# One hybrid decoder block on one core: when the rotary angles, tables and k's rotation are issued

## The chip, the cores and the metric

The kernel runs on one core of one Trainium2 chip. A core has a matrix engine (TensorE, here PE, with its weight loads as PEld), a vector engine (VectorE, DVE), a scalar engine (ScalarE, ACT), GpSimd (POOL) and a sync engine (SyncE, SP), which in this kernel issues nearly all DMA transfers. Each engine works through its own instruction list strictly in the order in which the program wrote it, and waits where an operand is not there yet. The metric is the device time of one execution in microseconds (us); lower is better.

## The reference

One decoder block in float32: RMSNorm with adaptive shift and scale, one large input projection, a sliding-window attention branch with rotary positions and learned sinks, a gated spatial branch with a LayerNorm, a gated merge, and an output projection with a second norm. Cut to what the change touches:

```python
def _rope(t, positions):
    inv_freq = ROPE_THETA ** (-jnp.arange(half) / half)
    ang = positions[..., None] * inv_freq
    cos, sin = jnp.cos(ang)[:, :, None, :], jnp.sin(ang)[:, :, None, :]
    t1, t2 = t[..., :half], t[..., half:]
    return jnp.concatenate([t1 * cos - t2 * sin, t2 * cos + t1 * sin], -1)
...
    h = _rms(x, g_pre) * (1.0 + scale) + shift
    q, k, v, z_a, u_b, v_b, z_b, g_logits = jnp.split(h @ w_in, SPLIT_IDX, -1)
    q, k = _rope(q, positions), _rope(k, positions)
...
    vn = _layernorm(v, ln_g, ln_b)      # v: gelu of v_b, in the gated spatial branch
```

The sequence is 2048 long and the model is 1024 wide; q has 8 heads and k and v have 2, of 64 columns each. All arrays are float32.

## The kernel before

**Products.** Every big matrix product is a Strassen-like scheme: for a pair of output column tiles seven half-size products stand in place of eight (`p` = 0 to 6). Each operand is split in a rounded high part and a low part, and one product is 12 matmuls of 128x512 (4 slices of the contraction, three of high-high, high-low and low-high each; `mm3`, L170). So a product needs a weight tile `W` (high by ACT, L223; low by DVE, L158, through `w_of` and `low_now`) and a moving tile `T` (high by ACT, L392 or L782; low by DVE, L803 and others). The sequence is done in two halves of 1024 (`s` = 0 and 1).

**The order of the work.** The program is written out product by product. `step` counts a slot up after each product; the text calls it the product's number, from 0. `later(n, f)` puts `f` in front of the product that is n slots on, `later(n, f, True)` behind its matmuls, and "mid" in their middle. Nothing is reordered afterwards: where `f` is called, its instructions enter the engines' lists.

**Products 0 to 27** are the first four pairs of the first half, done product by product over all four pairs at once: products 0 to 3 use moving tile `T[0]`, 4 to 7 `T[1]`, 8 to 11 `T[2]`, 12 to 15 `T[3]` (the fourth), 16 to 19 `T[4]`, 20 to 23 `T[5]`, 24 to 27 `T[6]`. In this stretch DVE also builds the moving tiles (L704, L762, L158) and sums the weight tiles. From product 28 on each pair takes seven products in a row: 28 to 34, 35 to 41, 42 to 48 and so on, in the four PSUM banks X, W, Y and Z.

**Rotary tables.** `rope_steps` (L583) is a generator of 21 short steps that reduce position times frequency to an angle; `rope_do(1)` runs one. Nine of them (DVE at L593, L623, L632, L590, L637; one of them is two ACT instructions, L625 and L626) run behind products 9 to 17. `rope_out` (L639) turns both angle tiles into sine and cosine on ACT and stores them to DRAM (`cs_s`, L646); the sine function needs a table that ACT loads first (ACT_TABLE_LOAD). `load_rope` (L861) loads them back as four tiles, sine and cosine for each half of the 1024 columns; each is four small DMAs on SP (L868, 32x512, called row loads below).

**k's rotation.** Pair 2 yields k (and v). Its results are stored raw (`kr_s`); `rope_finish` (L947) loads them again (L954, and L958 with rows swapped), multiplies by sine on POOL (`psub`, L161) and by cosine on DVE (L962), adds (L164), rounds (ACT, L966), takes the low part (L158) and stores (L990).

**LayerNorm of v_b.** `ln_step` (L920) loads a 128x512 block (SP, L923), PE transposes it behind a later product (L929, 4 matmuls of 128x128), then statistics and the norm follow on DVE (L933, L934, L941) with a power on POOL (L154, L155). For i = 0, 1, 2, 3 the load is called ahead of product 27, 29, 32, 34, and the transposes stand behind product 31, 33, 36, 38.

**Evacuation.** At p = 4 of a pair DVE adds bank Y to a kept tile (L436, shown as L164) and so frees bank Y, into which product p = 6 writes.

Of the kernel before, what the change touches and what calls it, by code (L numbers as in the profile page):

```python
# [50 lines left out]
NFIRST = 4  # L51
# [4 lines left out]
def hybrid_block(ctx: ExitStack, tc: tile.TileContext, xt, x, wada, wgate, wI, wP, wO,  # L56
# [30 lines left out]
    def flat(tag, dt=F32):  # L87
        return t2(tag, [P, 512], dt)
# [10 lines left out]
    def dram(name, shape):  # L99
        return tc.dram_tile(shape, F32, name=name)  # L100
# [16 lines left out]
    kr_s = [dram(f"kr{i}", [P, TG]) for i in range(2)]  # L117
# [39 lines left out]
    def sub(o, a, b):  # L157
        dve.tensor_tensor(out=o, in0=a, in1=b, op=ALU.subtract)  # L158

    def psub(o, a, b, op=ALU.subtract):  # L160
        pool.tensor_tensor(out=o, in0=a, in1=b, op=op)  # L161

    def add(o, a, b):
        dve.tensor_tensor(out=o, in0=a, in1=b, op=ALU.add)  # L164
# [64 lines left out]
    def later(n, f, post=False):  # L229
        hooks.setdefault((slot[0] + n, post), []).append(f)  # L230
# [419 lines left out]
    def rope_do(n):  # L650
        for _ in range(n):
            next(rope_it, None)
# [208 lines left out]
    def load_rope(s, ns):  # L861

        def one(h, i, key):
            g = 2 * s + h
            t = flat("m")
            for r in range(4):
                at = 64 * (r // 2) + r % 2
                sp.dma_start(t[at : at + 64 : 2, :] if at < 64 else t[at:P:2, :], cs_s[i][32 * g : 32 * (g + 1), :])  # L868
            if key == "s":
                later(3, lambda: act.activation(out=t, in_=t, func=AF.Copy, scale=col[:, C_SGN : C_SGN + 1]))  # L870
            ropet[key, h] = t
        for h in range(2):
            for i, key in enumerate("cs"):
                later(ns[2 * h + i], lambda h=h, i=i, key=key: one(h, i, key))
# [32 lines left out]
    def ft(key):  # L907
        return int(key[0]) - 1
# [38 lines left out]
    def rope_finish(h, R, put_out, wait, raw=None):  # L947
        st = {}

        def turn():  # L950
            nonlocal R
            if raw is not None:
                R = flat("x")
                sp.dma_start(R, raw)  # L954
            st["hi"] = flat("x", F32R)
            st["rot"] = st["hi"].bitcast(F32)
            for r in range(2):
                sp.dma_start(st["rot"][r:P:2, :], (R if raw is None else raw)[1 - r : P : 2, :])  # L958

        def mix():  # L960
            psub(st["rot"], st["rot"], ropet["s", h], ALU.mult)
            dve.tensor_tensor(out=R, in0=R, in1=ropet["c", h], op=ALU.mult)  # L962

        def both():
            add(R, R, st["rot"])
            act.copy(st["hi"], R)  # L966

        def low():
            sub(R, R, st["rot"])
        later(1 + wait, turn)  # L970
        later(5 + wait, mix)
        later(6 + wait, both, True)
        later(8 + wait, low)
        later(9 + wait, lambda: put_out(st["rot"], R))
# [8 lines left out]
    def ev_kv(s):  # L983
        def ev(key, src, psum):
            h = half(key)
            if ft(key) == 0:
                def put_out(hi, lo):
                    ks = slice(P + s * NT + h * 512, P + s * NT + (h + 1) * 512)
                    for i, t in enumerate((hi, lo)):
                        sp.dma_start(k_s[:, i, ks], t)  # L990
                R = rope_in(src, psum, "e")
                if s == 0:
                    store(1, kr_s[h], R)
                rope_finish(h, R, put_out, (15, 9)[h] if s == 0 else h, kr_s[h] if s == 0 else None)
            else:
                t = src
                if psum:
                    t = flat("e")
                    act.copy(t, src)

                def turn():
                    b = bank()
                    for c in range(4):
                        pe.transpose(b[:, c * P : (c + 1) * P], t[:, c * P : (c + 1) * P], ident)

                    def out_():
                        o = flat("qS"[s])
                        act.copy(o, b)
                        at = 1 + s * 8 + h * 4
                        store(1, v_s[:, at : at + 4, :], o.rearrange("p (a b) -> p a b", a=4))  # L1010
                    later(1, out_)
                later((3, 10)[h] if s == 0 else 2, turn, True)
        return ev
# [309 lines left out]
    def run_all():  # L1323
        nonlocal T

        for s in range(NS):
# [6 lines left out]
            if s == 0:  # L1333
                later(26, setup_sgu)
                later(28, zero_heads)
            load_rope(s, ((29, 28, 31, 30), (10, 11, 12, 13))[s])
            for i in range(8):
                later((27 + 5 * i // 2, 17 + 3 * i)[s], lambda i=i: ln_step(s, i))
            for c in range(4):
# [25 lines left out]
            if s == 0:  # L1365
# [50 lines left out]
                later(2 * NFIRST, fetch_all, True)  # L1416
                later(NFIRST, lambda: sp.dma_start(mcpt, mcp))
                later(NFIRST, lambda: sp.dma_start(snk8, sinks.broadcast_to([P, 8])))
                for i in range(9):
                    later(9 + i, lambda: rope_do(1), True)  # L1420
                later(26, rope_out, "mid")
                later(12, lambda: dve.tensor_scalar(out=snk8, in0=snk8, scalar1=1.0 / SM, scalar2=None, op0=ALU.mult))
                for p in range(3, 7):
                    for i, (n, post) in enumerate(((-4, True), (-3, False), (-3, True), (-2, False), (-2, True), (-1, False))):
# [218 lines left out]
```

## Time and profile before

| | us |
|---|---|
| three executions: median (lowest to highest) | 1201.62 (1200.4 to 1201.99) |
| the profiled execution | 1203.53 |
| its span, first to last instruction | 1201.8 |
| PE busy in the span | 1184.4 |
| mean granted clock of PE, share of full speed | 0.997 |

PE is busy nearly all the time, so the reading is of its short gaps: a timeline of PE shows where a product starts later than the one before it allows, and the timelines of DVE, ACT and SP show what it waited for. In a timeline a row merges neighbouring instructions of the same form: start, time from its start to its end, engine, line, operation, operands, count, and in brackets the idle time before it with the instruction that ended it. Matmuls of a row overlap the next row's first ones by some 0.15 us, so products are counted from start to start.

### The profile page before, as it was taken

What the parts mean: (1) busy time and instruction counts of PE and PEld (TensorE: products, weight loads), DVE (VectorE), ACT (ScalarE), POOL (GpSimd) and SP (SyncE); (2) the same over time, 40 slices, a digit from 0 to 9 for tenths busy, and PEclk for the clock granted to TensorE, in tenths of its full rate; (3) what the DMA queues carried; (4) which work ended last, traced back from release to release, by engine and by line L of the source; (5) the groups of instructions that cost most, each with busy time, mean ns of one, the idle gap of its engine ahead of it and who ended that gap; (6) DMA issues with size and microseconds to landing.
All of it is one profiled execution on the core that took longest, in us unless ns stands there. A gap on an engine that the chain in (4) does not pass through costs nothing.

```text
span 1201.8 us, 17373 instructions
## 1 busy us (share of the span) xinstructions
PE 1184.4 (99%) x5440; PEld 945.6 (79%) x5440; DVE 869.2 (72%) x1320; ACT 644.0 (54%) x1379; POOL 342.4 (28%) x290
## 2 busy tenths in 40 slices
PE   8999999999999999999999999999999999999997
PEld 4677878888777777888888887777778878888886
DVE  6897688678876676355866886554877977767775
ACT  5476455568765685443444766555845412444443
POOL 0001455333365201112201113130042301255453
PEclk9999999999999999999999999999999999999999
DMA  9546898959899997868779998998968987846352
GB/s 354 232 150 205 268 358 316 279 162 296 258 329 347 310 318 271 279 221 263 254 233 278 269 292 244 317 306 254 330 199 287 383 262 261 290 149 191 129 179 88
DMA packets 228548, 312.78 MB, mean 260 GB/s; under 512 B 20964, under 2 KB 103012, under 8 KB 228456
## 3 DMA queue, kind: packets, MB, share of 16 engines
q1 hardware_dynamic: 227984, 310.99, 79.5%
q8 instruction: 43, 0.70, 0.2%
q14 instruction: 49, 0.40, 0.1%
q0 software_dynamic: 176, 0.53, 0.1%
q10 hardware_dynamic: 296, 0.16, 0.1%
HBM read 201.82 MB, written 105.06 MB: 255 GB/s over the span
## 4 chain that ended last, share of the span: by engine, by line
PE 83%; DVE 6%; DMA 5%; ACT 2%; issue 2%; SPq 1%; POOL 0%; ACTq 0%; DVEq 0%; POOLq 0%
PE bankY L175 27%; PE bankX L175 19%; PE bankW L175 11%; PE bankZ L175 11%; PE b L175 3%; PE s L175 2%; PE b L1168 2%; PE s L1118 1%; PE s L1119 1%; DMA raw<-in_wP 1%; PE b L1057 1%; DVE W L158 1%; PE b L1153 1%; DMA raw<-sS 1%; DVE e L164 1%
## 5 line engine op out<-in xcount | busy, mean ns | idle before, releaser
L175 PE MATMUL bankY<-T,W 128*128 128x512 f32 x1566 | 383.2, 393 | 2.6 <-DVE e L164 2.3
L175 PEld LDWEIGHTS bankY<-T,W 128*128 128x128 f32 x1566 | 291.7, 188 | 64.3 <-issue 3.7
L158 DVE TENSOR_TENSOR W<-raw,W 128x512 fp32r<-128x512 f32 x327 | 268.5, 827 | 73.4 <-ACT W L223 70.5
L223 ACT CAST W<-raw 128x512 fp32r<-128x512 f32 x327 | 201.8, 618 | 131.0 <-PE b L175 41.9
L175 PE MATMUL bankX<-T,W 128*128 128x512 f32 x1098 | 266.9, 391 | 0.1
L175 PEld LDWEIGHTS bankX<-T,W 128*128 128x128 f32 x1098 | 204.2, 188 | 41.9 <-DVE T L803 0.5
L175 PE MATMUL bankW<-T,W 128*128 128x512 f32 x672 | 165.7, 393 | 2.9 <-DVE T L158 2.0
L175 PE MATMUL bankZ<-T,W 128*128 128x512 f32 x672 | 163.8, 391 | 0.0
L175 PEld LDWEIGHTS bankW<-T,W 128*128 128x128 f32 x672 | 124.4, 188 | 32.7 <-DVE T L158 3.5
L175 PEld LDWEIGHTS bankZ<-T,W 128*128 128x128 f32 x672 | 124.9, 188 | 27.2 <-ACT T L392 1.6
L161 POOL TENSOR_TENSOR S<-x,x 128x512 f32<-128x512 f32 x28 | 37.1, 1329 | 239.1 <-DMA x<-yb 107.8
L161 POOL TENSOR_TENSOR raw<-raw,raw 128x512 f32<-128x512 f32 x46 | 73.9, 1606 | 93.1 <-DVE W L158 44.3
L161 POOL TENSOR_TENSOR S<-raw,raw 128x512 f32<-128x512 f32 x23 | 34.9, 1518 | 168.8 <-DMA raw<-in_wI 74.5
L158 DVE TENSOR_TENSOR T<-x,T 128x512 fp32r<-128x512 f32 (+1 forms) x105 | 73.6, 748 | 3.6 <-ACT T L392 3.6
L164 DVE TENSOR_TENSOR e<-bankY,e 128x512 f32<-128x512 f32 x43 | 29.7, 690 | 59.2 <-PE bankY L175 59.0
L175 PE MATMUL b<-T,W 128*128 128x512 f32 x282 | 69.7, 390 | 0.5 <-DVE W L158 0.5
L175 PEld LDWEIGHTS b<-T,W 128*128 128x128 f32 x282 | 52.8, 188 | 11.8 <-DVE W L158 0.9
L175 PE MATMUL s<-T,W 128*128 128x512 f32 x246 | 60.1, 389 | 0.2 <-DVE e L164 0.2
L392 ACT CAST T<-x 128x512 fp32r<-128x512 f32 x100 | 56.0, 619 | 3.8 <-PE s L175 2.1
L175 PEld LDWEIGHTS s<-T,W 128*128 128x128 f32 x246 | 46.1, 188 | 10.2 <-issue 0.6
L161 POOL TENSOR_TENSOR raw<-S,raw 128x512 f32<-128x512 f32 x23 | 32.7, 1424 | 70.1 <-DVE W L158 58.5
L1147 ACT ACTIVATE P<-P,rc 128x128 f32<-128x128 f32 x128 | 44.5, 396 | 11.6 <-DVE rc L1143 11.6
(292 smaller groups left out, 1459.0 us busy)
## 6 DMA issues: line engine op xcount, KB each, us to landing
raw<-in_wI SPq DMA_DIRECT2D x127, 256.0 KB, 4.6
raw<-sS SPq DMA_DIRECT2D x92, 256.0 KB, 5.0
g<-e SPq DMA_DIRECT2D x64, 256.0 KB, 4.1
sS<-raw SPq DMA_DIRECT2D x43, 256.0 KB, 4.4
T<-in_wada SPq DMA_DIRECT2D x16, 512.0 KB, 8.2
q<-q SPq DMA_DIRECT2D x64, 128.0 KB, 5.4
q<-k_s SPq DMA_DIRECT2D x64, 128.0 KB, 4.9
raw<-m SPq DMA_DIRECT2D x32, 256.0 KB, 4.1
```

The source lines that it names most:

```text
L158: dve.tensor_tensor(out=o, in0=a, in1=b, op=ALU.subtract)
L161: pool.tensor_tensor(out=o, in0=a, in1=b, op=op)
L164: dve.tensor_tensor(out=o, in0=a, in1=b, op=ALU.add)
L175: pe.matmul(o, w[:, i, sl], t[:, j, kt, :], start=start and kt == kts[0] and n == 0, stop=stop and kt == last and n == 2, skip_group_check ...
L223: act.copy(w[:, 0, :], src)
L392: act.copy(T[p][:, 0, kt, :], rs[kt])
L1057: pe.matmul(b[:, ch * P : (ch + 1) * P], st["v", h][:, ch, :], wT[:, c, :], start=True, stop=True)
L1118: pe.matmul(o, q[:, g, :], k[:, 0, :], start=True, stop=False)
L1119: pe.matmul(o, q[:, g, :], k[:, 1, :], start=False, stop=True)
L1147: act.activation(out=st["P", kv][:, g, 0:P], in_=st["P", kv][:, g, 0:P], func=AF.Copy, scale=st["rc", kv][:, g : g + 1])
L1153: pe.transpose(t[:, g * P : (g + 1) * P], st["P", kv][:, g, 0:P], ident)
L1168: pe.matmul(o[own, :], v[:, k, own], st["pv", kv][k], start=k == 1, stop=k == 0)
```

## The change

- The nine angle steps run behind products 13 to 21 in place of 9 to 17.
- `low_now` is called once more, ahead of product 9: the low part of the weight tile of product 11 is then issued at once, ahead of two of the vector instructions that prepare the fourth moving tile.
- `rope_out` runs in the middle of product 24 in place of 26.
- The four table loads of the first half are called ahead of products 27, 26, 29, 28 in place of 29, 28, 31, 30.
- `rope_finish` for k in the first half starts two products sooner (wait 13 and 7 in place of 15 and 9).

```diff
-                rope_finish(h, R, put_out, (15, 9)[h] if s == 0 else h, kr_s[h] if s == 0 else None)
+                rope_finish(h, R, put_out, (13, 7)[h] if s == 0 else h, kr_s[h] if s == 0 else None)
...
-            load_rope(s, ((29, 28, 31, 30), (10, 11, 12, 13))[s])
+            load_rope(s, ((27, 26, 29, 28), (10, 11, 12, 13))[s])
...
+                later(2 * NFIRST + 1, low_now)
                 for i in range(9):
-                    later(9 + i, lambda: rope_do(1), True)
-                later(26, rope_out, "mid")
+                    later(13 + i, lambda: rope_do(1), True)
+                later(24, rope_out, "mid")
```

The number of instructions is the same on every engine but ACT, which loads a function table 35 times in place of 34 (the added one stands ahead of the first exponential of the attention, L1138). PE's list is the same. Names below carry tile numbers that shift with the order of allocation.

DVE's list before, from the second of the four instructions (L704) that scale the source of the fourth moving tile; `W_794` is the weight tile of product 11, `W_839` that of product 12:

```order
L704 SCALAR_TENSOR_TENSOR x_357<-x_357,AS,e_489 128x512
L593 SCALAR_TENSOR_TENSOR T_321<-T_321 128x512
L704 SCALAR_TENSOR_TENSOR x_358<-x_358,AS,e_489 128x512
L803 SCALAR_TENSOR_TENSOR T_823<-x_356,AS,T_823 128x512
L158 TENSOR_TENSOR W_794<-x_406,W_794 128x512
L158 TENSOR_TENSOR W_839<-S_830,W_839 128x512
```

DVE's list of the change from the same place, where the weight tile of product 12 is `W_838`:

```order
L158 TENSOR_TENSOR W_794<-x_406,W_794 128x512
L704 SCALAR_TENSOR_TENSOR x_357<-x_357,AS,e_489 128x512
L704 SCALAR_TENSOR_TENSOR x_358<-x_358,AS,e_489 128x512
L803 SCALAR_TENSOR_TENSOR T_824<-x_356,AS,T_824 128x512
L158 TENSOR_TENSOR W_838<-S_830,W_838 128x512
```

The low part of product 11's weights went up by four places, and the angle step L593 went out to a later place.

ACT's list before, from the weight cast of product 27; `m_1002` and `m_1001` are the two angle tiles, L916 is the gelu that empties bank W:

```order
L223 CAST W_1177<-raw_1062 128x512
L916 ACTIVATE e_1192<-bankW 128x512
L223 CAST W_1195<-raw_1085 128x512
L916 ACTIVATE e_1210<-bankZ 128x512
L223 CAST W_1216<-S_1213 128x512
L643 ACT_TABLE_LOAD
L643 ACTIVATE m_1002<-m_1002 128x512
L645 ACTIVATE m_1001<-m_1001,col 128x512
```

ACT's list of the change from the same cast:

```order
L223 CAST W_1177<-raw_1057 128x512
L643 ACT_TABLE_LOAD
L643 ACTIVATE m_1100<-m_1100 128x512
L645 ACTIVATE m_1099<-m_1099,col 128x512
L916 ACT_TABLE_LOAD
L916 ACTIVATE e_1196<-bankW 128x512
L223 CAST W_1199<-raw_1081 128x512
L916 ACTIVATE e_1214<-bankZ 128x512
```

The two sines stand four instructions further up, with a table load on either side of them.

SP's list before, from the first of the four sets of row loads (L868); `q_1308` is the LayerNorm block i = 1, and L954 and L958 load k's first half:

```order
L868 DMA m_1274<-cs_315 32x512 x4
L254 DMA sS_1_95<-raw_1085 128x512
L911 DMA g_0_254<-e_1261 128x512
L868 DMA m_1303<-cs_314 32x512 x4
L923 DMA q_1308<-vb_302 128x4x128
L246 DMA raw_1335<-in_wI 128x512
L868 DMA m_1337<-cs_315 32x512 x4
L1192 DMA S_1342<-in_x 128x512
L1192 DMA S_1344<-in_x 128x512
L954 DMA x_1346<-kr_312 128x512
L958 DMA x_1348<-kr_312 64x512 x2
```

SP's list of the change from the third set of row loads on (the first two stand further up); `q_1323` is the same LayerNorm block:

```order
L868 DMA m_1284<-cs_315 32x512 x4
L954 DMA x_1289<-kr_312 128x512
L958 DMA x_1291<-kr_312 64x512 x2
L254 DMA sS_1_95<-raw_1081 128x512
L911 DMA g_0_254<-e_1271 128x512
L868 DMA m_1318<-cs_314 32x512 x4
L923 DMA q_1323<-vb_302 128x4x128
L246 DMA raw_1351<-in_wI 128x512
```

All four sets of row loads and the three loads of k's first half now stand ahead of the LayerNorm block i = 1, where two sets stood before.

## Rows read from the trace of the kernel before

**Rows 1.** The page: busy time of each engine with its share of the span.

```profile
PE 1184.4 (99%) x5440; PEld 945.6 (79%) x5440; DVE 869.2 (72%) x1320; ACT 644.0 (54%) x1379; POOL 342.4 (28%) x290
```

**Rows 2.** Timeline of PE: first row of products 11, 12, 16, 17, 24 and 25.

```profile
68.04 0.61 PE L175 MATMUL b<-T,W 128*128 128x512 f32 x2
...
71.52 2.88 PE L175 MATMUL bankX<-T,W 128*128 128x512 f32 x12
...
82.40 2.43 PE L175 MATMUL bankW<-T,W 128*128 128x512 f32 x10
...
85.86 2.92 PE L175 MATMUL bankZ<-T,W 128*128 128x512 f32 x12
...
105.29 1.87 PE L175 MATMUL bankW<-T,W 128*128 128x512 f32 x7
...
109.78 2.89 PE L175 MATMUL bankZ<-T,W 128*128 128x512 f32 x12
```

**Rows 3.** Timeline of PE: the transposes of LayerNorm block i = 1, and products 34, 40, 41 and 42.

```profile
136.61 0.60 PE L929 MATMUL b<-cst,q 128*128 128x128 f32 x4
136.97 2.98 PE L175 MATMUL bankY<-T,W 128*128 128x512 f32 x12
...
154.35 2.88 PE L175 MATMUL bankZ<-T,W 128*128 128x512 f32 x12
159.56 4.44 PE L175 MATMUL bankY<-T,W 128*128 128x512 f32 x12 [2.34 <-DVE e L164]
...
164.33 3.01 PE L175 MATMUL bankX<-T,W 128*128 128x512 f32 x12
```

**Rows 4.** Busy time of each engine in two stretches of 2 us, with the count of instructions, PE's granted clock (PEclk, 1.00 is 2.4 GHz and 0.50 is 1.2 GHz), the busy share of the DMA engines and GB/s.

```profile
157.00:159.00 2.00, 0.23 (x2) 0.00 (x0) 1.97 (x5) 0.00 (x0) 0.07 (x1) 1.00 1.08 392
161.00:163.00 2.00, 2.00 (x7) 1.51 (x6) 2.00 (x4) 0.19 (x1) 1.37 (x2) 0.50 1.06 341
```

**Rows 5.** The same view for the two stretches in which DVE builds the moving tiles; the busy times are of PE, PEld, DVE, ACT and POOL in this order.

```profile
65.00:90.00 25.00, 24.08 (x106) 19.20 (x105) 24.61 (x42) 19.08 (x31) 0.00 (x0) 1.00 0.50 168
90.00:109.00 19.00, 18.08 (x77) 13.82 (x75) 18.57 (x27) 10.48 (x18) 3.48 (x2) 1.00 0.63 208
```

**Rows 6.** Timeline of DVE: the low parts of the weights of products 11 and 12, an angle step with idle time ahead of it, and the last low part of the seventh moving tile.

```profile
68.37 0.69 DVE L158 TENSOR_TENSOR W<-x,W 128x512 fp32r<-128x512 f32 x1
69.05 0.69 DVE L158 TENSOR_TENSOR W<-S,W 128x512 fp32r<-128x512 f32 x1
...
77.07 0.69 DVE L593 SCALAR_TENSOR_TENSOR T<-T 128x512 f32<-128x512 f32 x1 [0.39 <-ACT T L626]
...
108.47 0.68 DVE L158 TENSOR_TENSOR T<-x,T 128x512 fp32r<-128x512 f32 x1
```

**Rows 7.** Timeline of ACT: the cast of the weights of product 12, that of product 27, the sines' table load, the first sine, and a copy out of bank Z behind the first exponentials, where the change adds a table load.

```profile
68.39 0.62 ACT L223 CAST W<-S 128x512 fp32r<-128x512 f32 x1 [1.10 <-DMA S<-in_wI]
...
110.33 0.60 ACT L223 CAST W<-raw 128x512 fp32r<-128x512 f32 x1
...
113.83 1.28 ACT L643 ACT_TABLE_LOAD   x1
115.13 0.63 ACT L643 ACTIVATE m<-m 128x512 f32<-128x512 f32 x1
...
233.25 0.57 ACT L445 COPY bankZ<-bankY 128x512 f32<-128x512 f32 x1 [0.85 <-PE bankY L175]
```

**Rows 8.** Timeline of SP's issues: the two table stores, LayerNorm block i = 0, the first set of row loads, block i = 1, the third set, the loads of k's first half, the fourth set.

```profile
115.79 0.93 SPq L646 DMA_DIRECT2D cs<-m  x2
...
117.72 0.76 SPq L923 DMA_DIRECT2D q<-vb  x1
...
122.46 2.42 SPq L868 DMA_DIRECT2D m<-cs  x4
...
128.45 0.59 SPq L923 DMA_DIRECT2D q<-vb  x1
...
129.75 2.36 SPq L868 DMA_DIRECT2D m<-cs  x4
...
133.24 0.43 SPq L954 DMA_DIRECT2D x<-kr  x1
133.72 1.12 SPq L958 DMA_DIRECT2D x<-kr  x2
...
135.99 2.63 SPq L868 DMA_DIRECT2D m<-cs  x4
```

**Rows 9.** Time from issue to landing in us, lowest, median and highest: of the six LayerNorm loads between 110 and 165 us, then of block i = 1 alone; and, with the median in the last column, of the v_b stores and the table stores between 110 and 120 us and of the row loads between 118 and 165 us.

```profile
DMA to landing us min/median/max: 2.9/4.5/5.3
...
DMA to landing us min/median/max: 3.9/3.9/3.9
...
vb<-e SPq DMA_DIRECT2D x2, 256.0 KB, 4.3
cs<-m SPq DMA_DIRECT2D x2, 256.0 KB, 3.8
...
m<-cs SPq DMA_DIRECT2D x16, 64.0 KB, 2.4
```

**Rows 10.** Timeline of DVE: the statistics of LayerNorm block i = 1, and the add that empties bank Y ahead of product 41.

```profile
139.73 0.69 DVE L933 BATCH_NORM_STATS2 bst<-b 128x6 f32<-128x512 f32 x1
...
158.76 0.66 DVE L164 TENSOR_TENSOR e<-bankY,e 128x512 f32<-128x512 f32 x1
```

## The prediction

> **What bounds the kernel now.** I read the page first: PE is busy for 1184.4 of 1201.8 us [rows 1], so a change pays only where it closes or opens one of PE's gaps. Next I read PE's timeline from start to start. A product that nothing delays takes 2.72 us to the next one's start, and a group of four 128x128 transposes 0.36 (136.61 to 136.97) [rows 3]. By that measure product 11 loses 71.52 - 68.04 - 2.72 = 0.76 us, product 16 loses 0.74 and product 24 loses 1.77 [rows 2]. Product 41 should start at 154.35 + 2.72 = 157.07 and starts at 159.56, 2.49 late, with DVE's add as the releaser. From there to product 42, with one group of transposes between, 4.77 us pass where 3.08 would do, 1.69 too many [rows 3]. The windows say why: in the wait PE has 0.23 of 2 us busy, and two us after its end the granted clock is 0.50, the 1.2 GHz level [rows 4]. So this one wait costs 4.18 us in all. Last I read what stood behind each of them: the lists of DVE, ACT and SP.
>
> **Angle steps and the extra low part.** They move work on DVE, which in this stretch is the bound: 24.61 of 25 us busy from 65 to 90, 18.57 of 19 from 90 to 109 [rows 5]. Product 11's weights get their low part at 68.37 [rows 6], and product 11 waits for it. The order shows it four places earlier, so the 0.76 at product 11 goes, and with the angle steps out of the way so does the 0.74 at 16. But the moving steps and the low part stay on the same engine, and all nine angle steps still come ahead of the last low part of the seventh tile (108.47), which holds product 24. From the scaling of the fourth tile to there DVE has the same 67 instructions in both lists. The end of that row of work, not the waits within it, sets product 25. So the 1.50 us reappear as a longer wait at product 24, about 1.77 + 1.50 = 3.3.
>
> What is left is how DVE's idle time changes. It was 0.39 + 0.43 = 0.82 over the two stretches [rows 5], and 0.39 of that is one angle step that waits for ACT's pair [rows 6]. With the step L593 (0.69) no longer ahead, DVE reaches the low part of product 12 at about 69.05 - 0.69 = 68.36, while its cast runs from 68.39 to 69.01 [rows 7]: some 0.56 new. ACT's angle pair comes to stand ahead of the fifth-group tile's cast, an estimated 0.55 by the pair's two instructions, the nearest row being that 0.39. Net +1.11 - 0.39 = +0.7 if the other 0.43 stays, +0.3 if a later DVE finds those operands ready. I take +0.3, since DVE is the later one at each of them; bounds -0.8 (all old idle gone, none new) and +0.7. Product 25 then starts 0.3 later.
>
> **Sines and row loads.** ACT's list shows the sines directly behind product 27's cast, which ended at 110.93 [rows 7]. With the 0.3, the table load of 1.28 and a sine of 0.63 the first sine is done near 113.2 (before: 115.76). Its store is issued at once, as it was (115.79) [rows 8], and lands 3.8 later [rows 9], near 117.1. There SP begins the first set of row loads, which began at 122.46 before [rows 8].
>
> The price stands on SP. LayerNorm block i = 1, issued at 128.45 before, has all four sets and k's three loads ahead of it now: one more set of 2.36, another of 2.63, and 0.43 + 1.12 for k's loads [rows 8], 6.5 us with their gaps of about 0.1 each some 6.8. To count it from the new start: SP issues two sets, and between them a v_b store and a weight load of some 0.4 each, and comes to block i = 0 at 117.1 + 4.8 + 0.8 = 122.7. That block waits for the v_b store, issued near 119.8 and 4.3 in landing [rows 9]: it goes out at 124.1, done at 124.9. From its end to block i = 1 passed 128.45 - 118.48 = 9.97 before [rows 8], two sets among them; now the same stretch holds two sets again, and k's loads, 1.6 with their gaps: 124.9 + 10.0 + 1.6 = 136.5. I take 136.4; bounds 133 (by 128.45 + 6.8 less what the earlier start gives back, without the wait for the store) and 137.
>
> The block landed 3.9 after its issue, of six 2.9 to 5.3 [rows 9]. So it is there at 140.3, bounds 136 and 142.3. PE comes to its transposes at 136.61 + 0.3 = 136.9 [rows 3]. **A new wait of 3.4 us stands there.** Everything of PE behind it is queued: transposes, product 34 at 140.7.
>
> **The old wait at product 41.** From 136.97 to 164.33 less 4.18 is 23.18 us from product 34 to 42 with no wait [rows 3]. Product 41 would come to bank Y at 140.7 + (157.07 - 136.97) = 160.8. Is DVE's add done by then? It ran from 158.76 to 159.42, 19.03 after the statistics of block i = 1 began [rows 10]. Those now start at 140.8 or so, and DVE's list from there holds two instructions fewer (an add of about 0.7 and a multiply of about 1.2, since k's work stands further up). Even at 18 us, with 0.66 for the add, it is done near 159.5. So the old wait is gone: the two waits don't add up, the earlier covers the later. Product 42 starts at 140.3 + 0.36 + 23.18 = 163.8, 0.5 earlier than 164.33.
>
> **The clock.** PE's wait of 2.49 was followed by a stretch at 0.50 that cost 1.69 [rows 3, 4]. A wait of 3.4 in the same kind of work most likely does the same, after product 33: +1.69. Product 42 at 165.5, +1.2. Bounds 0 (the clock holds) and 2.3 (1.69 in the proportion 3.4 to 2.49). The wait of about 3.3 at product 24 may be followed by the same; that is hidden, since the block's landing decides what comes later.
>
> **At nothing.** The sines' table load comes ahead of the evacuations of banks W and Z and of weight casts, so those come some 3.9 later (two tables at 1.28, a sine pair); bank Y and bank X are written next and the cast of product 28 has two products of cover. If that is gone it costs up to 3.9 there, which again precedes the wait for the block. The added table load stands ahead of the first exponential; ACT idles 0.85 for PE just behind it [rows 7], so 0.4 us of its 1.28 could reach a copy and PE waits for none of these. k's multiply on DVE is queued ahead of bank Y's add for product 34 and waits for row loads landing near 133; without that cover product 34 would be held, but the block holds it longer. k's stores come earlier, and nobody waits for them.
>
> The sum against the profiled execution is 1203.53 + 1.2 = 1204.7 (span 1201.8, 1.73 around it); that execution lies 1.91 above the median of 1201.62, so the forecast is 1201.62 + 1.2 = 1202.8.
>
> **Two rules of the Trainium skill.** SP's four row loads take 2.42 to issue, 0.6 each, and land in 2.4 [rows 8, 9]; one issue is a quarter of a landing. The Trainium skill, page "DMA: Bandwidth & Descriptors", section "Issuing engines are not separate DMA queues", holds that the time to initiate a DMA is "usually small relative to the DMA itself". By that the order of SP's list would hardly matter and the second rival below would hold; the rows speak against it here, since twenty issues of 0.4 to 0.76 in a row come to over 10 us.
> The sine follows its table load's start by 1.30 us [rows 7]. The Trainium skill, page "ScalarE: Activation LUTs", section on what ACT_TABLE_LOAD costs, gives 1283 ns and a drain of 1380 ns, 2.66 us in all. By that the store, the block and the end would come 1.4 later (an estimate by that page, 1204.2); the row shows no such drain.
>
> **The rivals.** *One, the clock holds.* The wait is there but no slow stretch follows. For it: product 24's wait of 1.77 was followed by a product 25 of full speed [rows 2]. Against it: [rows 4]. Time: -0.5, so 1201.1. Chance 0.23.
> *Two, the queue doesn't bite.* SP's issues come closer together, or the row loads start earlier, and the block lands by 136.9. Then product 41's wait decides: with DVE ahead of its old time by 1.2 to 2.5 the old wait is 0 to 1.3, and the 1.69 goes with it. Time: 0.3 - 4.18 + (0 to 1.3), so -2.6 to -3.9, 1197.7 to 1199.0. Chance 0.17. For it: k's work does move away from the stretch ahead of 158.76. Against it: the count of issues.
> *Three, slower.* The block is issued at 137 and lands 5.3 later, at 142.3, in a queue that holds more transfers at once. Product 42 is then at 142.3 + 23.54 + 1.69 = 167.5, +3.2: 1204.8. The mechanism is that of the forecast; it makes the kernel slower than a measurement's width from a landing of 141.5 on. For it: the DMA engines are fully busy in [rows 4] and 5.3 was measured; against it: 3.9 for this very block. Chance 0.16.
> *Four, term one isn't neutral.* It can shift product 25 by -0.8 to +0.7, but the end moves only with the store, so it lies in the ranges above. That the change does nothing it says is excluded by the order lists.
>
> **How the numbers follow.** Forecast 0.45 at 1202.8 (by itself 1201.6 to 1204.0), rivals 0.22, 0.17 and 0.16. A measurement of this kernel tells about 0.2%, 2.4 us, from no change: below 1199.2 is faster, above 1204.0 slower. The range 1198.9 to 1204.8 leaves out most of rival two (0.12) and the upper half of rival three (0.08). Faster: rival two, 0.17. Slower: rival three and a little of the forecast, 0.18. The rest, 0.65, lies between.
>
> **What would show it.** Right: products 11 and 16 without a gap and a longer one at 24, released by DVE; the first row loads on SP near 117 and block i = 1 near 136.4; a gap of about 3.4 us ahead of PE's transposes L929 with that DMA as the releaser, a granted clock near 0.5 behind it; product 41 without a wait. The forecast is wrong if that gap is missing (SP ran faster than its rows), if product 41 still waits for DVE (the two waits add up), or if product 25 starts more than 0.8 earlier (DVE wasn't the bound of the tiles).

## The result and the profile after

| | before | changed |
|---|---|---|
| median of 20 executions, us | 1201.13 | 1204.63 |
| ratio of the times, 95% interval | | 1.0024 (1.0016 to 1.0033) |
| profiled execution, us (span) | 1203.53 (1201.8) | 1202.67 (1201.0) |

The changed kernel is slower by 0.24%, 2.9 us (1.9 to 4.0). One execution of 4232.68 us that was disturbed is left out of the ratio; without it the median of the changed kernel is 1204.35. The two profiled executions stand the other way round: that of before lies 2.4 over its median, that of the change is the lowest of its 20. So the profiles are read for places here, and their spans aren't compared.

Timeline of PE of the changed kernel: first row of product 20, product 21, product 24 (three rows) and 25, then the transposes of LayerNorm block i = 1, products 34, 40 and 41.

```profile
92.69 2.43 PE L175 MATMUL bankX<-T,W 128*128 128x512 f32 x10
...
96.11 2.92 PE L175 MATMUL bankY<-T,W 128*128 128x512 f32 x12
...
104.31 1.75 PE L175 MATMUL bankW<-T,W 128*128 128x512 f32 x7
107.68 0.96 PE L175 MATMUL bankW<-T,W 128*128 128x512 f32 x3 [1.62 <-DVE T L158]
108.88 0.73 PE L175 MATMUL bankW<-T,W 128*128 128x512 f32 x2 [0.24 <-DVE T L158]
109.45 2.90 PE L175 MATMUL bankZ<-T,W 128*128 128x512 f32 x12
...
139.48 0.63 PE L929 MATMUL b<-cst,q 128*128 128x128 f32 x4 [3.04 <-DMA q<-vb]
139.86 3.01 PE L175 MATMUL bankY<-T,W 128*128 128x512 f32 x12
...
157.28 2.88 PE L175 MATMUL bankZ<-T,W 128*128 128x512 f32 x12
161.93 3.01 PE L175 MATMUL bankY<-T,W 128*128 128x512 f32 x12 [1.76 <-DVE e L164]
...
165.12 2.98 PE L175 MATMUL bankX<-T,W 128*128 128x512 f32 x12
```

Against [rows 2, 3]: product 25 starts at 109.45 (109.78 before). Product 24 loses 5.14 - 2.72 = 2.42 in place of 1.77, product 20 loses 0.70 in place of 0.34. New is the idle time of 3.04 ahead of the transposes, released by the block's DMA. The wait at product 41 is still there: 161.93 in place of 157.28 + 2.72 = 160.00.

Timeline of SP's issues of the changed kernel: the table stores, the first set of row loads, block i = 0, k's first half, the fourth set, block i = 1, k's second half.

```profile
112.58 0.93 SPq L646 DMA_DIRECT2D cs<-m  x2
...
116.49 2.43 SPq L868 DMA_DIRECT2D m<-cs  x4
...
124.01 0.58 SPq L923 DMA_DIRECT2D q<-vb  x1
...
130.80 0.59 SPq L954 DMA_DIRECT2D x<-kr  x1
...
133.70 2.48 SPq L868 DMA_DIRECT2D m<-cs  x4
136.23 0.59 SPq L923 DMA_DIRECT2D q<-vb  x1
...
138.47 0.43 SPq L954 DMA_DIRECT2D x<-kr  x1
```

Against [rows 8] the row loads begin 6.0 us sooner, block i = 1 goes out 7.8 later, and k's first half gains only 2.4.

Timeline of DVE of the changed kernel: k's multiply for the first half, a weight's low part, k's multiply for the second half, the statistics of block i = 1, and the add that empties bank Y.

```profile
133.78 0.99 DVE L962 TENSOR_TENSOR x<-x,m 128x512 f32<-128x512 f32 x1 [4.97 <-DMA x<-kr]
...
139.64 0.69 DVE L158 TENSOR_TENSOR W<-S,W 128x512 fp32r<-128x512 f32 x1
143.19 0.69 DVE L962 TENSOR_TENSOR x<-x,m 128x512 f32<-128x512 f32 x1 [2.87 <-DMA x<-kr]
143.80 0.69 DVE L933 BATCH_NORM_STATS2 bst<-b 128x6 f32<-128x512 f32 x1
...
161.12 0.66 DVE L164 TENSOR_TENSOR e<-bankY,e 128x512 f32<-128x512 f32 x1
```

Here is what the forecast hadn't seen. The transposes begin at 139.48 and product 34 at 139.86, but DVE begins the statistics at 143.80: ahead of them in its list stands the multiply of k's second half, whose load was issued at 138.47 and which starts at 143.19. That load was issued 1.4 sooner than before (139.90) and came no sooner: it landed 4.6 after its issue, where it took 3.1 before (5.3 and 4.3 in second profiles of the two). From the statistics to the add 17.32 us pass, and product 41 waits for that add.

### The profile page after: what moved, and what is told of

The parts are those of the page before. It is cut to its first block, busy times and chain, and to the rows that moved or that the text cites. A ratio compares the mean times of both kernels' runs of the same rounds, so it can differ in the third digit from the quotient of the medians.

```text
span 1201.0 us, 17377 instructions
## 1 busy us (share of the span) xinstructions
PE 1181.3 (98%) x5440; PEld 944.5 (79%) x5440; DVE 860.1 (72%) x1320; ACT 645.6 (54%) x1380; POOL 350.2 (29%) x290
## 4 chain that ended last, share of the span: by engine, by line
PE 86%; DVE 5%; DMA 4%; ACT 2%; issue 1%; SPq 0%; POOL 0%; ACTq 0%; DVEq 0%; POOLq 0%
PE bankY L175 28%; PE bankX L175 19%; PE bankW L175 12%; PE bankZ L175 11%; PE b L175 4%; PE s L175 3%; PE b L1168 2%; PE s L1118 1%; PE s L1119 1%; PE b L1057 1%; DVE W L158 1%; PE b L1153 1%; DMA sS<-S 1%; DVE x L158 1%; ACT W L223 1%
## 5 line engine op out<-in xcount | busy, mean ns | idle before, releaser
L158 DVE TENSOR_TENSOR W<-raw,W 128x512 fp32r<-128x512 f32 x327 | 264.8, 815 | 73.8 <-ACT W L223 70.0
L161 POOL TENSOR_TENSOR S<-x,x 128x512 f32<-128x512 f32 x28 | 37.8, 1357 | 238.6 <-DMA x<-yb 108.0
L161 POOL TENSOR_TENSOR raw<-raw,raw 128x512 f32<-128x512 f32 x46 | 73.3, 1593 | 89.6 <-DVE W L158 39.5
L161 POOL TENSOR_TENSOR S<-raw,raw 128x512 f32<-128x512 f32 x23 | 38.4, 1671 | 175.1 <-DMA raw<-in_wI 68.8
L164 DVE TENSOR_TENSOR e<-bankY,e 128x512 f32<-128x512 f32 x43 | 29.7, 690 | 58.4 <-PE bankY L175 54.6
L158 DVE TENSOR_TENSOR T<-x,T 128x512 fp32r<-128x512 f32 (+1 forms) x105 | 69.1, 707 | 2.6 <-ACT T L392 2.5
L161 POOL TENSOR_TENSOR raw<-S,raw 128x512 f32<-128x512 f32 x23 | 32.7, 1423 | 68.7 <-DVE W L158 53.8
```

## The experiments

In every profile below the same five numbers are read, and the table puts them together: the start of the statistics of block i = 1 (DVE), of the add that empties bank Y, the idle time that the profile gives ahead of product 41, the start of product 42, and the ratio of the times to before. The start of product 42 also holds up to some 1 us of differences from the program's start, which vary with the execution.

| kernel | statistics | add | idle at 41 | product 42 | ratio (95%) |
|---|---|---|---|---|---|
| before | 139.73 | 158.76 | 2.34 | 164.33 | 1 |
| before, second profile | 138.25 | 157.99 | 1.94 | 161.99 | 1 |
| changed | 143.80 | 161.12 | 1.76 | 165.12 | 1.0024 (1.0016 to 1.0033) |
| changed, second profile | 144.06 | 161.41 | 2.62 | 167.00 | |
| tables and k sooner only | 143.91 | 161.23 | 0.32 | 165.21 | 1.0016 (1.0006 to 1.0026) |
| angle steps and low part only | 138.73 | 156.09 | none | 160.25 | 1.0001 (0.9990 to 1.0012) |
| changed, block i = 1 loaded first | 146.10 | 163.37 | 3.31 | 168.95 | 1.0027 (1.0017 to 1.0038) |
| changed, k's second half back | 140.69 | 159.90 | none | 164.71 | 1.0015 (1.0005 to 1.0025) |
| changed, all of k back | 142.41 | 161.86 | 4.34 | 167.98 | 1.0038 (1.0024 to 1.0053) |
| the same, block i = 1 first | 141.48 | 161.06 | 3.14 | 167.83 | 1.0035 (1.0022 to 1.0048) |
| before, k seven products later | 138.85 | 155.37 | none | 160.97 | 0.9993 (0.9982 to 1.0004) |
| before, k four products later | 138.65 | 155.17 | none | 160.77 | 0.9985 (0.9973 to 0.9996) |
| changed, k four products later than before | 137.79 | 155.13 | none | 160.73 | 1.0004 (0.9993 to 1.0015) |

**The two halves of the change, each alone.** Tables and k's rotation only:

```diff
-                later(2 * NFIRST + 1, low_now)
-                    later(13 + i, lambda: rope_do(1), True)
+                    later(9 + i, lambda: rope_do(1), True)
```

> Only the tables and k's rotation sooner (sines in product 24, row loads and k's rotation two products sooner); angle steps behind products 9 to 17 and no extra low part, as before. Theory one (SP's order makes two waits: PE for LayerNorm block i = 1, and DVE for k's second half, whose multiply stands ahead of that block's statistics): block i = 1 issued at 135.5 to 136.5, 2.5 to 3.5 us of wait ahead of its transposes, 1.5 to 2.5 at product 41, product 42 within 0.6 of 165.1, time 2 to 3.5 us over before. Theory two (the moved angle steps and the low part cost the time on DVE): time equal to before within 1 us.

Angle steps and low part only:

```diff
-                later(24, rope_out, "mid")
+                later(26, rope_out, "mid")
-            load_rope(s, ((27, 26, 29, 28), (10, 11, 12, 13))[s])
+            load_rope(s, ((29, 28, 31, 30), (10, 11, 12, 13))[s])
-                rope_finish(h, R, put_out, (13, 7)[h] ...
+                rope_finish(h, R, put_out, (15, 9)[h] ...
```

> Only the angle steps behind products 13 to 21 and the extra low part ahead of product 9; sines, row loads and k's rotation as before. Theory one: products 11 and 16 lose nothing, product 24 loses 1.77 + 1.5 = about 3.3, product 25 starts within 0.5 of 109.8, no wait ahead of the transposes of block i = 1, product 41 waits as before (2 to 3), time within 1 us of before. Theory two: 2 to 3 us over before.

The first is slower by 0.16%, the second equals before: the cost lies in the tables and k's rotation (the 0.08% between the first and the whole change lies within their intervals). In the first the block went out at 136.47, as expected, and the wait is there, but the granted clock fell behind it (0.50 from 140 to 142) and the wait at product 41 shrank to 0.32. Timeline of PE of that kernel: the transposes of block i = 1, products 34, 35 and 41.

```profile
139.78 1.09 PE L929 MATMUL b<-cst,q 128*128 128x128 f32 x4 [3.09 <-DVE e L164]
140.52 3.92 PE L175 MATMUL bankY<-T,W 128*128 128x512 f32 x12
144.28 2.88 PE L175 MATMUL bankX<-T,W 128*128 128x512 f32 x12
...
162.04 2.98 PE L175 MATMUL bankY<-T,W 128*128 128x512 f32 x12 [0.32 <-DVE e L164]
```

Product 34's row lasts 3.92 in place of 3.01, and product 42 (165.21) is where it is in the changed kernel without that slow stretch (165.12): PE only came later to a wait that it had anyway. The profile names DVE's add as the releaser of the transposes; that add ended at 139.66, and the block landed at about the same time (136.47 and 3.2 for the landing), so the name decides nothing between them. With k's second half back the transposes began before that add had ended (139.51 and 139.57), so the block is the likelier one. In the second kernel product 25 started at 109.87 with 1.64 idle in product 24, so the angle steps only shift the waits, and product 41 found no wait in this execution.

**Loading block i = 1 first.** Its load moves behind that of block i = 0, its transposes stay:

```diff
-        later(4, turn, True)
+        d = 2 if s == 0 and i == 1 else 0
+        later(4 + d, turn, True)
...
-                later((27 + 5 * i // 2, 17 + 3 * i)[s], lambda i=i: ln_step(s, i))
+                later((27 if i == 1 else 27 + 5 * i // 2, 17 + 3 * i)[s], lambda i=i: ln_step(s, i))
```

> The changed kernel with the load of LayerNorm block i = 1 issued right behind that of block i = 0, ahead of two sets of row loads and k's loads; its transposes stay behind product 33. Theory one (DVE's wait for k's second half sets product 41 anyway): no wait ahead of the transposes, product 41 waits 4.5 to 5.5, product 42 at 164.5 to 165.6, time within 1 us of the changed kernel. Rival (the wait of 3.04 for the block is the cost): product 42 at 161.5 to 162.6, time 2.5 to 3.5 us below the changed kernel.

Timeline of DVE of that kernel: k's multiplies for both halves; then of PE: the transposes of block i = 1 and product 41.

```profile
136.30 0.69 DVE L963 TENSOR_TENSOR x<-x,m 128x512 f32<-128x512 f32 x1 [6.64 <-DMA x<-kr]
...
145.49 0.69 DVE L963 TENSOR_TENSOR x<-x,m 128x512 f32<-128x512 f32 x1 [2.13 <-DMA x<-kr]
```

```profile
138.93 0.63 PE L929 MATMUL b<-cst,q 128*128 128x128 f32 x4 [1.64 <-issue]
...
164.18 4.56 PE L175 MATMUL bankY<-T,W 128*128 128x512 f32 x12 [3.31 <-DVE e L164]
```

The block's DMA is no longer the releaser ahead of the transposes, yet nothing is won: 1.0027 against 1.0024. Expected was that they don't wait at all; 1.64 stayed, and the profile names no releaser for it. What ends just before is work of DVE on PSUM (L891, until 138.82) that stands in its list behind k's first half, which held DVE until 136.30; that this is the cause is likely and not shown. k's loads went out 2.6 later than in the changed kernel (133.43 in place of 130.80 for the first half), though the load put ahead of them takes only some 0.6 of SP, and DVE's statistics began 2.3 later (146.10). Product 41 waited 3.31 and not 4.5 to 5.5, and product 42 came at 168.95 and not at 164.5 to 165.6: the next block's transposes waited 0.83 for their load, and the clock fell behind product 41 (0.50 from 166 to 168). So the theory's places weren't met here, but its time was. The wait for the block wasn't the cost by itself.

**k's second half back by two products.**

```diff
-                rope_finish(h, R, put_out, (13, 7)[h] ...
+                rope_finish(h, R, put_out, (13, 9)[h] ...
```

> The changed kernel with the second half of k's rotation two products later, as in the kernel before (7 back to 9); the first half stays sooner. Theory one: the wait of about 3 ahead of the transposes of block i = 1 stays, DVE's statistics of that block follow it within 1 us, product 41 waits under 0.5, product 42 at 162.9 to 163.6, time 1.5 to 2.5 us below the changed kernel. Rival (other work of DVE sets product 41): its wait stays at 1.5 to 2.5 and the time within 1 us of the changed kernel.

Timeline of DVE of that kernel, the statistics and the add; then of PE, products 34, 35 and 41.

```profile
140.69 0.69 DVE L933 BATCH_NORM_STATS2 bst<-b 128x6 f32<-128x512 f32 x1
...
159.90 0.66 DVE L164 TENSOR_TENSOR e<-bankY,e 128x512 f32<-128x512 f32 x1
```

```profile
140.03 4.46 PE L175 MATMUL bankY<-T,W 128*128 128x512 f32 x12
144.33 2.91 PE L175 MATMUL bankX<-T,W 128*128 128x512 f32 x12
...
161.63 2.89 PE L175 MATMUL bankY<-T,W 128*128 128x512 f32 x12
```

The statistics follow the transposes at once and product 41 has no wait, as theory one has it. Part of that is the slow stretch ahead of it: product 34 took 4.30 and the transposes 0.52, where they took 2.82 and 0.36 before, and without these 1.64 PE would have come to product 41 at 159.99, some 0.6 ahead of the end of DVE's add (160.56). So most of the second wait goes with k's second half, and it isn't shown that all of it does. The gain is 1.1 us (1.0015 against 1.0024, intervals that overlap) and not 2: in this execution the clock fell behind the first wait (idle 2.72), and product 42 came at 164.71 and not at 163.

**All of k back, and the same with block i = 1 first.**

```diff
-                rope_finish(h, R, put_out, (13, 7)[h] ...
+                rope_finish(h, R, put_out, (15, 9)[h] ...
```

> The changed kernel with both halves of k's rotation where they were before (wait 15 and 9); angle steps, sines and row loads stay as changed. Theory one (k's multiplies on DVE, queued ahead of their data, hold DVE, and k's loads hold SP): block i = 1 is issued about 1.8 sooner than in the changed kernel, at 134.0 to 134.8, the wait ahead of its transposes falls to 0.8 to 2.0, DVE runs ahead of it without a wait for k's data, product 41 waits 0 to 1.5; product 42 at 161.2 to 163.2, time 0 to 1.5 us over before. Rival (the row loads alone cost it all): wait 3.0 again and time 2 to 3 us over before.

> The kernel of e7 with the load of block i = 1 right behind that of block i = 0 besides, transposes where they were. Theory one: no wait ahead of the transposes, no wait of DVE for k's data ahead of them; product 41 as in the kernel before, product 42 at 160.0 to 163.5, time within 1 us of before. Rival (any earlier row loads cost 2 us or more): time 2 us or more over before.

Both have the highest ratios of all, though their intervals overlap that of the changed kernel, and theory one as I had put it falls: it gave 0 to 1.5 us over before for the one and within 1 us for the other, and 4.6 and 4.2 came, as the rivals had it, by which sooner row loads cost that much by themselves. Timeline of DVE of the first: a weight's low part, k's multiply for the first half, the statistics; then of SP, the load of k's first half; then of PE, product 41.

```profile
138.52 0.68 DVE L158 TENSOR_TENSOR W<-S,W 128x512 fp32r<-128x512 f32 x1
141.80 0.69 DVE L962 TENSOR_TENSOR x<-x,m 128x512 f32<-128x512 f32 x1 [2.60 <-DMA S<-in_x]
142.41 0.69 DVE L933 BATCH_NORM_STATS2 bst<-b 128x6 f32<-128x512 f32 x1
```

```profile
135.99 0.43 SPq L954 DMA_DIRECT2D x<-kr  x1
```

```profile
162.67 5.12 PE L175 MATMUL bankY<-T,W 128*128 128x512 f32 x12 [4.34 <-DVE e L164]
```

The wait for the block is gone here, and DVE waits nonetheless: the load of k's first half goes out at 135.99, 2.75 later than before [rows 8], because the fourth set of row loads now stands ahead of it, and lands 5.7 after that. (The releaser that the profile names, `S<-in_x`, is another load, issued at 135.04; the multiply starts within 0.1 of the landing of k's.) k's multiply again keeps the statistics back, and all the work of k stands between them and the add (19.45 us). So the theory needs one more term: a row load that is issued sooner is paid by what SP issues later, and whichever half of k stands ahead of the statistics hands that on to DVE.

**k later than before.** This turns the change round, and the last kernel keeps the tables sooner:

```diff
-                rope_finish(h, R, put_out, (15, 9)[h] ...
+                rope_finish(h, R, put_out, (22, 16)[h] ...
```

> The kernel before with k's rotation seven products later (wait 22 and 16 in place of 15 and 9), nothing else; the other way than the change moved it. If product 41 waits because k's multiplies, adds and low parts stand on DVE between the statistics of block i = 1 and the add that empties bank Y (17 to 20 us from the one to the other in every profile so far): about 6 us of that go, no wait at product 41, product 42 at 159.6 to 160.5, time 1 to 2.5 us below before. Rival (the work only moves the wait to the next pair): product 42 there as well, but a wait of 1 us or more at product 48 or 55 and time within 1 us of before.

With (19, 13) in that place:

> The kernel before with k's rotation four products later (wait 19 and 13). By the same theory about half of k's work still stands ahead of the add: the wait at product 41 under 1 us, time 0.5 to 2 us below before; by the rival within 1 us of before.

With (19, 13) in the changed kernel:

> The changed kernel with only k's rotation moved, to four products later than in the kernel before (wait 19 and 13); angle steps, sines and row loads stay sooner. If the cost lies in k's multiplies, which stand on DVE ahead of the statistics of block i = 1 while their data is still under way: DVE doesn't wait ahead of those statistics, they begin at 137.5 to 139.5, the add that empties bank Y starts before 157, no wait at product 41, product 42 at 159.8 to 161.5, time 0 to 2 us below before. Rival (row loads that are issued sooner cost time by themselves, as the two kernels with k put back suggest): time 2 us or more over before.

In all three the statistics begin at 137.8 to 138.9, the add is done by 156.1, and product 41 doesn't wait. Timeline of PE of the last kernel, the transposes of block i = 1, products 40 to 42 and product 44; its timeline of ACT, a rounding of k's ahead of product 44; then PE of the kernel with k seven products later, its next large wait, at product 48.

```profile
137.13 0.63 PE L929 MATMUL b<-cst,q 128*128 128x128 f32 x4 [0.84 <-DVE e L164]
...
154.93 2.88 PE L175 MATMUL bankZ<-T,W 128*128 128x512 f32 x12
157.65 2.88 PE L175 MATMUL bankY<-T,W 128*128 128x512 f32 x12
...
160.73 2.98 PE L175 MATMUL bankX<-T,W 128*128 128x512 f32 x12
...
169.00 3.02 PE L175 MATMUL bankY<-T,W 128*128 128x512 f32 x12 [1.63 <-ACT bankY L445]
```

```profile
166.72 0.62 ACT L966 CAST x<-x 128x512 fp32r<-128x512 f32 x1 [2.41 <-DVE x L164]
```

```profile
180.63 0.70 PE L175 MATMUL bankY<-T,W 128*128 128x512 f32 x2 [1.76 <-DVE e L164]
```

Product 41's wait goes, and part of it comes back further on. With k seven products later it does so one pair on, as the rival had it. With k four products later product 44 waits 1.66 and, with the tables sooner, 1.63, for ACT's copy out of bank Y: ahead of that copy ACT rounds k's results (L966) and has waited 2.41 for DVE's add.

With the tables sooner and k out of the way the time is that of before (1.0004), 2.4 us under the changed kernel by the ratios, with intervals that don't overlap: the place of k's rotation carries most of the cost. (Its loads, its multiplies and what follows them move together, so these aren't told apart.) Up to 2 us below before was expected; that didn't come. And the sooner tables aren't free. With k where it was they cost 0.38% (1.0038 against 1); with k four products later 0.19% (1.0004 against 0.9985), which is barely clear of the noise. The profile of the last kernel shows 0.84 of that: block i = 1 was issued at 133.84, where it went out at 128.85 with the tables left alone, and its transposes wait. (DVE's add, the releaser named, ended at 137.02; a landing 3.2 after the issue, as above, comes at the same time.) The profiled execution is the fastest of the 12 of this kernel, 1200.80 with a median of 1203.31, so what the others lose is not seen. Four products later with the tables left alone is the only version here with all its work that is faster than before, by 0.15% (0.04 to 0.27), one of eleven kernels that were timed against it.

**Is DVE the bound of products 11 to 24?** This kernel leaves out six of the nine angle steps, so its angles are others:

```diff
-        stt(r, n1, D1B, r)
-        stt(r, n0, D0B, r)
-        dve.tensor_tensor(out=a, in0=s, in1=r, op=ALU.add)
...
-        stt(s, a, -P1, s)
-        stt(r, a, -P2, r)
-        dve.tensor_tensor(out=r, in0=s, in1=r, op=ALU.add)
```

> The kernel before without six of the nine angle steps on DVE that run behind products 9 to 17 (the other three stay, so the angles and both rotations come out otherwise). If DVE is the bound of products 11 to 24: 6 times 0.69 = 4.1 us less work, the 3.6 us lost at products 11, 16, 20 and 24 go nearly all, product 25 at 106.0 to 107.0, time 2.5 to 4 us below before. Rival (casts of ACT or weight loads bound it): product 25 at 108.5 or later, time within 1.2 us of before.

It is faster by 0.16% (0.07 to 0.25), 1.9 us, between the two. Timeline of DVE of that kernel, the two largest waits:

```profile
69.25 0.69 DVE L158 TENSOR_TENSOR W<-S,W 128x512 fp32r<-128x512 f32 x1 [0.74 <-ACT W L223]
...
77.83 0.75 DVE L797 SCALAR_TENSOR_TENSOR T<-q,DS,T 128x512 fp32r<-128x512 f32 x1 [1.56 <-ACT T L776]
```

Of the 4.1 us taken out 2.3 come back as waits for ACT's casts, and product 25 starts at 108.26. So DVE bounds the stretch at first, and ACT stands right behind it; product 25 came between the two expectations (106.0 to 107.0, or 108.5 and later).

**Second profiles.**

> The kernel before once more, for one more profile: whether the wait of 2.49 at product 41 and the stretch at half the clock behind it are there in each execution. If they are: product 42 at 164.0 to 164.7. If they come and go: product 42 between 160.2 (no wait) and 162.5 (a wait without the clock).

> The changed kernel once more, for a second profile. If the waits belong to the kernel: 2.5 to 3.5 us ahead of the transposes of block i = 1, product 41's wait 1.5 to 2.5 where the clock holds after the first wait and under 1 where it falls; product 42 between 164.5 and 166.5 either way. If they come and go with the execution: below 163.

In the second profile of before product 41 waits 1.94 and the clock holds (product 42 at 161.99). In that of the change both waits are there, 2.40 and 2.62, and the clock falls behind the second: product 42 at 167.00, half a microsecond over the bound that I gave. Timeline of PE of that second profile, the transposes of block i = 1 and product 41; then the busy time and the granted clock, read as in [rows 4], behind the first wait in the first profile of the change, behind the second in its second profile, and behind the first with k's second half back.

```profile
138.96 0.63 PE L929 MATMUL b<-cst,q 128*128 128x128 f32 x4 [2.40 <-DMA q<-vb]
...
162.22 4.59 PE L175 MATMUL bankY<-T,W 128*128 128x512 f32 x12 [2.62 <-DVE e L164]
```

```profile
140.00:142.00 2.00, 2.00 (x10) 1.64 (x10) 0.33 (x1) 0.32 (x1) 0.00 (x0) 1.00 0.98 339
...
164.00:166.00 2.00, 2.00 (x7) 1.56 (x6) 2.00 (x4) 0.00 (x0) 1.56 (x1) 0.56 0.98 301
...
141.00:143.00 2.00, 2.00 (x6) 1.58 (x5) 0.56 (x2) 1.59 (x5) 0.76 (x2) 0.50 1.05 403
```

The mean start of product 42 is 163.16 for before and 166.06 for the change, 2.9 apart as the 20 executions are, but that agreement is chance: the mean spans of the same profiles, 1200.5 and 1201.9, are 1.4 apart, in good part since the first profile of before loses 1.3 to 1.7 near 950 to 966 that the other three don't. Two profiles each show the places of the waits, not the size of the difference.

## Why the prediction was right or wrong

The time came out inside the range and on the slower side, as forecast; the size was off, 2.9 us (1.9 to 4.0) where 1.2 stood. By the prediction's own sign, product 41 still waiting for DVE, its account of that product was wrong. That product 42 came at 165.12, close to the 165.5 of the forecast, is luck: a second wait of 1.93 that was to be gone stood in the place of a slow clock of 1.69 that was to come. The size is close to that of rival three (+3.2), but not by its mechanism: the block landed 3.1 after its issue, not 5.3.

- **Angle steps and low part: right in kind.** Products 11 and 16 lost their waits (67.92 to 70.64 and 81.81 to 84.53, 2.72 each), 20 and 24 lost more, but 24 lost 2.42 and not 3.3. Product 25 came at 109.45 and 109.57 against 109.78 and 109.39; counted from the start of product 11, which takes out differences from the program's start, that is 0.21 and 0.35 sooner, where 0.3 later stood with bounds of -0.8 and +0.7. The new idle time of DVE was 0.57 for product 12 and 0.39 behind ACT's pair, where 0.56 and 0.55 stood. Alone, this part is 1.0001.
- **Sines, SP, the block: right.** The row loads began at 116.49 (117.1 forecast), the block went out at 136.23 (136.4), the idle time was 3.04 and 2.40 (3.4).
- **"So the old wait is gone": wrong, and the step that failed.** The statistics of block i = 1 were to start "at 140.8 or so" and started at 143.80: the list behind it has the multiply of k's second half ahead of the statistics, and I had priced its place (two instructions fewer behind) but not its data, whose load SP issued at 138.47 and which landed 4.6 later, near 143.1. The two waits don't cover each other; both stay, 3.04 and 1.93. The kernel with k's second half put back shows it: there the statistics begin at 140.69, and of the second wait some 0.6 would be left at full clock. Whether SP's order or the DMA engines kept that load back wasn't separated: the engines' busy share is 1.07, 0.98 and 1.05 in the three stretches of 2 us from 138 to 144.
- **The 4.18 us at product 41 in before: mis-sized.** 1.69 of it was the slow stretch of one execution. The second profile of before has the wait (1.94) and no slow stretch. So less could be won there than the sum said, and this term, more than any other, makes the 1.2 too small: the same 165.5 lies 3.5 behind the 161.99 of the second profile.
- **The clock: half right.** In the first profile of the change nothing followed the 3.04 (clock 1.00); in the second the fall came behind product 41's wait (0.56). Where it came in the executions without a profile isn't known. Over its executions the mean granted clock is 0.997, over those of before 0.998; a stretch like that of [rows 4], some 3.4 us at 0.50, makes 0.0014 of a 1200 us span. (Rival one, in which the clock holds, stands with a chance of 0.23 and of 0.22; the chances add up with 0.22.)
- **At nothing: right here.** I wrote that k's multiply could hold bank Y's add but that the block would hold product 34 longer. DVE did stand idle for 4.97 ahead of the multiply, and the add ended at 137.2, some 0.6 after PE could have come to product 34 (133.56 + 2.72 + 0.36 = 136.64); the block held it until 139.86.

## What to carry to other kernels

Moving a consumer up an in-order list is worth nothing unless its data moves too: look for what is queued behind it, and follow that to the product that waits for it. A saturated issuing engine, or saturated DMA engines behind it, has no sooner, only a different order, and each load that goes ahead is paid by the ones behind it. Where one wait seems to cover another, check that nothing else behind the same late loads starts the second afresh. And take the base of a sum from more than one profiled execution.

## What wasn't expected of the hardware

- The fall of the clock comes and goes. Idle times of 3.04 and 2.40 ahead of the transposes and of 1.94 and 1.76 at product 41 were not followed by one; 2.72 and 3.09 ahead of the transposes and 2.34, 2.62, 3.14, 3.31 and 4.34 at product 41 were, in work that is nearly the same. What decides it isn't settled.
- The same list of DVE took between 17.4 and 19.7 us from the statistics to the add (17.36 with only the angle steps moved, 19.03 and 19.74 in two executions of before), so the wait at product 41 itself varies from none to 2.34 with the same order on DVE from there on. The traces show what stretches single instructions: one that starts beside a multiply or add of POOL (L161) can take 1.78 in place of 0.69. k's multiply on DVE with POOL's nearest, in the first profile of before and then in the second:

```profile
138.02 1.79 DVE L962 TENSOR_TENSOR x<-x,m 128x512 f32<-128x512 f32 x1
137.68 1.58 POOL L161 TENSOR_TENSOR x<-x,m 128x512 f32<-128x512 f32 x1 [0.94 <-DMA x<-kr]
...
137.65 0.69 DVE L962 TENSOR_TENSOR x<-x,m 128x512 f32<-128x512 f32 x1
138.19 1.29 POOL L161 TENSOR_TENSOR x<-x,m 128x512 f32<-128x512 f32 x1 [1.82 <-DMA x<-kr]
```

In the first POOL had begun 0.34 sooner, in the second DVE was ahead of it. From 100 to 400 us of the first profile 83 such instructions of DVE (L158, L164, L962, no PSUM bank among their operands) ran while POOL did none of L161, and none took over 1.05; of 62 that met one, 20 took about 1.78. No kernel was built to take POOL's work away, so how much of the 17.4 to 19.7 it makes isn't measured.
